# Attention heads in pairs on halves of the array, with the distance term in a loaded table

## The chip, the cores and the metric

The kernel runs on one core of a Trainium2 chip. A core has a matrix engine (TensorE, in the profile PE, with its weight loads listed apart as PEld), a vector engine (VectorE, DVE), a scalar engine (ScalarE, ACT), a general engine (GpSimd, POOL), a queue engine (SyncE, SP) and 16 DMA engines. PE multiplies a stationary tile (it lies on the array's rows and columns) with a moving tile and adds into PSUM; the other engines read PSUM and work on SBUF. The metric is device time in microseconds (us).

## The reference

Two layers of a decoder, for 256 tokens of width 1024 in f32. Each layer normalizes, projects to the inputs of four token mixers, gates and merges them, and projects out; then comes a dense feed-forward (layer 0) or one with 8 experts of which each token uses 2 (layer 1). The attention is the part that matters here; `q`, `k` and `v` have 8 heads of 64:

```python
h = rmsnorm(x, norm_mix[l])
z = h @ w_in[l]
z_a, z_b, z_q, z_k, z_v, z_d = jnp.split(z, IN_SPLITS, axis=-1)
...
scores = jnp.einsum('brnqhd,brnkhd->brnqhk', qb, kk, ...) / math.sqrt(dh)
alibi = -slopes[None, :, None] * (dist * dilation).astype(jnp.float32)[:, None, :]
scores = jnp.where(valid[:, :, None, :], scores + alibi, MASK_VALUE)
m = jnp.max(scores, axis=-1, keepdims=True)
p = jnp.exp(scores - m)
den = jnp.sum(p, axis=-1)
o = jnp.einsum('brnqhk,brnkhd->brnqhd', p, vv.astype(jnp.float32)) / den[..., None]
```

This is done for three pairs of window and dilation, whose outputs are mixed by a softmax of their denominators. Over 256 tokens that is one softmax over all earlier keys, in which a key counts as often as configurations reach it: each score gets the head's distance term, −slope × distance, and the logarithm of that count (−1e30 for a count of zero).

## The kernel before, in words

**Weights.** SP loads the f32 weights in tiles of 1 MB (`raw`, L133). `split` turns each half into two rounded parts: ACT copies the high part (`whi`, L172), DVE subtracts it for the low one (`wlo`, L173). A projection in the mixers is then two matmuls per 128 × 128 block: `whi` with both parts of the activations (512 columns, L249) and `wlo` with the high one (256 columns, L251). The feed-forward stages use three matmuls (L164 to L166). PE runs these streams back to back from weight tile to weight tile.

**The mixer of a layer** (`mixer_layer`, L273) is a list of units, each of them a piece of such a projection. Two side generators are fed in between the units: `first_side` (gating unit, pooling, convolution of 31 steps) and `attention` (L465). After each unit `pump` advances them by a rate: from the sixth unit on 2.2 steps of `first_side` and 1.6 of `attention`. What comes out is a program order; a scheduler then lays out each engine's instructions from it, with waits on semaphores where tiles come free or results are needed. In the kernel before it mixes attention's matmuls one by one into the projection.

**Attention** goes head by head in a pipeline of three steps.

- `scores` (L470): for each half `t` of the queries a matmul of 64 rows, queries stationary and keys moving (L476, 128 and 256 columns), then a matmul of two rows in bf16 (L478), which adds the distance term from the small table `al` into the same PSUM. Both halves of one head share one PSUM bank (`pss`).
- `softmax` (L482): DVE scales the scores and adds `lc`, the logarithm of the count, which is a part of the tile `mc` (L484); then the row maximum (L490), the exponential on ACT (L492), the reciprocal (L494), and the scaling of the two halves. `turned` (L499) transposes the three blocks on PE (L502), and ACT copies them out (L504).
- `values` (L507): two matmuls of 64 columns (L511 with 256 moving columns, L513 with 128). Even heads write PSUM rows 0 to 63, odd heads rows 64 to 127 of the same tile `po`.

Heads of even number lie on rows 0 to 63 of the `qT` and `kT` tiles, those of odd number on rows 64 to 127. In the loop of L518 head `i` has its scores taken while head `i − 1` is turned and head `i − 2` meets its values. The PSUM tiles of attention come from a pool with four banks.

**Small tables.** `small_loads` (L282) issues on POOL's queue, once for each layer, the small parameters (`sm`, L284), four more and `mc` (L290), in layer 0 also `al` and `cst`. After them POOL masks a part of `sm` (L303), while DVE halves a bias from it (`hb`, L301).

Of the kernel before, what the change touches and what calls it, by code (L numbers as in the profile page):

```python
# [2 lines left out]

# [2 lines left out]

# [4 lines left out]

F32 = mybir.dt.float32
F32R = mybir.dt.float32r
BF16 = mybir.dt.bfloat16
I32 = mybir.dt.int32
AF = mybir.ActivationFunctionType
ALU = mybir.AluOpType
# [2 lines left out]
P = 128  # L20
D = 1024
T = 256
# [3 lines left out]
HEADS = 8  # L26
HD = 64
# [15 lines left out]
C_LT = C_IOTA + 256  # L43
C_KEY = C_LT + 64
C_END = C_KEY + 8
M_LC = 0
M_PA = M_LC + 384
M_END = M_PA + 4 * 272


# [12 lines left out]
def shape_constants():  # L63
    c = np.zeros((P, C_END), np.float32)
    m = np.zeros((P, M_END), np.float32)
    i = np.arange(P)

    q = np.arange(T)[:, None]
    k = np.arange(T)[None, :]
    dist = q - k  # L70
    cnt = np.zeros((T, T))
    for window, dil in ((128, 1), (512, 4), (2048, 16)):
        cnt += (dist >= 0) & (dist <= window) & (dist % dil == 0)
    lc = np.where(cnt > 0, np.log(np.maximum(cnt, 1)), -1e30).astype(np.float32)
    m[:, M_LC:M_LC + 128] = lc[:P, :P]
    m[:, M_LC + 128:M_LC + 384] = lc[P:]
# [15 lines left out]
    al = np.zeros((P, 3, T), ml_dtypes.bfloat16)  # L92
    for h in range(HEADS):
        s = 8.0 * 2.0 ** (-8.0 * (h + 1) / HEADS)
        o = 32 * (h % 4)
        al[o, h // 4] = -s * np.arange(T)
        al[o + 1, h // 4] = s
        al[o, 2] = 1.0
        al[o + 1, 2] = np.arange(T)
    return c, m, al  # L100


@with_exitstack
def decoder_kernel(ctx, tc, x_in, consts_in, mconsts_in, alibi_in, small_in, gln_in, gbs_in, norms_in, w_in,
                   w_br_a, w_br_b, w_br_c, w_br_d, w_gate, w_out, dense_w1, dense_w3, dense_w2,
                   router_in, moe_w, out):
    nc = tc.nc
    cp = ctx.enter_context(tc.tile_pool(name="cp", bufs=1))
# [4 lines left out]
    psB = ctx.enter_context(tc.tile_pool(name="psB", bufs=4, space=bass.MemoryType.PSUM))  # L113
# [57 lines left out]
    def split(hi, lo, src):  # L171
        return (nc.scalar.activation(hi, src, AF.Copy),  # L172
                nc.vector.tensor_tensor(out=lo, in0=src, in1=hi.bitcast(F32), op=ALU.subtract))  # L173


    x = cp.tile([P, TT, D], F32, name="x")
# [17 lines left out]
    al = cp.tile([P, 3, T], BF16, name="al")  # L194

    def sqrt_table(after, rows=slice(None)):

# [75 lines left out]
    def mixer_layer(l, h):  # L273
        with ExitStack() as lctx:
# [7 lines left out]
            def small_loads():  # L282
                q = nc.gpsimd
# [5 lines left out]
                                        ap=[[0, 64], [1, P]]))  # L289
                q.dma_start(mc, mconsts_in)  # L290
                if l == 0:
                    q.dma_start(al, alibi_in)
                    q.dma_start(cst, consts_in)

            mean_w = lp.tile([P, P], F32, name="mean_w")
# [168 lines left out]

            def attention():  # L465
                yc = y_tile("c", 4, "yc", "y4", 1)
                lc = mc[:, M_LC:M_LC + 384]
                po = None

                def scores(hd):  # L470
                    j, r = hd // 2, slice((hd % 2) * 64, (hd % 2) * 64 + 64)
                    ps = psB.tile([P, 384], F32, name="pss", tag="ax")
                    for t in range(TT):
                        o = ps[:, 0:128] if t == 0 else ps[:, 128:384]
                        nk = P * (t + 1)
                        nc.tensor.matmul(o, lhsT=qT[r, j, t * P:(t + 1) * P], rhs=kT[r, j, 0:nk], start=True, stop=False)  # L476
                        ar = slice(32 * (hd % 4), 32 * (hd % 4) + 2)
                        nc.tensor.matmul(o, lhsT=al[ar, hd // 4, t * P:(t + 1) * P], rhs=al[ar, 2, 0:nk],  # L478
                                         start=False, stop=True)
                    return ps  # L480

                def softmax(ps):  # L482
                    s = wk.tile([P, 384], F32, name="s", tag="s", bufs=2)
                    nc.vector.scalar_tensor_tensor(out=s, in0=ps, scalar=1.0 / math.sqrt(HD), in1=lc,  # L484
                                                   op0=ALU.mult, op1=ALU.add)
                    nm = wk.tile([P, TT], F32, name="nm", tag="nm", bufs=3)
                    den = wk.tile([P, TT], F32, name="den", tag="den", bufs=3)
# [16 lines left out]
                    nc.scalar.activation(pr, pT, AF.Copy)  # L504
                    return pr

                def values(hd, pr, po):  # L507
                    r = slice((hd % 2) * 64, (hd % 2) * 64 + 64)
                    if po is None:
                        po = psB.tile([P, T], F32, name="po", tag="ax")  # L510
                    nc.tensor.matmul(po[r, :], lhsT=v[:, 0, hd * HD:(hd + 1) * HD], rhs=pr[:, 0:256],  # L511
                                     start=True, stop=False, skip_group_check=True)
                    nc.tensor.matmul(po[r, 128:256], lhsT=v[:, 1, hd * HD:(hd + 1) * HD], rhs=pr[:, 256:384],  # L513
                                     start=False, stop=True, skip_group_check=True)
                    if hd % 2 == 1:
                        split(yc[0][:, hd // 2], yc[1][:, hd // 2], po)
                        po = None
                    return po  # L518

                ps, sf, pr = {}, {}, {}  # L520
                for i in range(HEADS + 2):
                    if i >= 2:
                        po = values(i - 2, pr.pop(i - 2), po)
                        yield
                    if 1 <= i <= HEADS:
                        pr[i - 1] = turned(sf.pop(i - 1))
                        yield
                    if i < HEADS:
                        sf[i] = softmax(scores(i))
                        yield  # L530

            def evac_v(t, ps):
                nc.scalar.activation(v[:, t], ps, AF.Copy)
# [63 lines left out]
            order[13:13] = [(lambda: branch_unit("a", w_br_a, 2, True, False), (2.2, 1.6))]  # L597
            order[18:18] = [(lambda: branch_unit("b", w_br_b, 2, False, False), (2.2, 1.6))]
            for un, r in order:
                un()  # L600
                pump(*r)
# [445 lines left out]
    ps = None  # L1047
# [8 lines left out]
def layouts(inputs):  # L1056

    f = {k: np.ascontiguousarray(np.asarray(v)) for k, v in inputs.items()}
    L = DEPTH
    consts, mconsts, alibi = shape_constants()  # L1060
    small = np.empty((L, P, S_END), np.float32)
    for l in range(L):
        s = small[l]
# [16 lines left out]
    moe_w = np.ascontiguousarray(np.concatenate(tiles, axis=3))  # L1080
    gln = np.stack([f["gmlp_ln_g"], f["gmlp_ln_b"]], axis=1).reshape(L, 512)
    return {
        "x": f["x"][0], "consts": consts, "mconsts": mconsts, "alibi": alibi, "small": small, "gln": gln, "gbs": f["gmlp_b_s"],
        "norms": norms, "w_in": f["w_in"], "w_br_a": f["w_br_a"], "w_br_b": f["w_br_b"], "w_br_c": f["w_br_c"],
        "w_br_d": f["w_br_d"], "w_gate": f["w_gate"], "w_out": f["w_out"], "dense_w1": f["dense_w1"],
        "dense_w3": f["dense_w3"], "dense_w2": f["dense_w2"], "router": f["moe_router"], "moe_w": moe_w,
# [21 lines left out]
```

## Time and profile before

| | before |
|---|---|
| median of 3 runs | 1617.06 us (1616.21 to 1619.08) |
| profiled execution | 1616.96 us |
| its span | 1615.1 us |
| granted clock of PE, mean | 0.987 |
| matmuls of attention in the two layers | L476 and L478: 32 each; L511 and L513: 16 each; transposes L502: 48 (of L476, L511 and L513, in plain f32, the profile lists two passes each) |

The span is what the profiler sees between the first and the last instruction; the time of an execution has a little around it. In rows of the page's groups an engine and a line are followed by output and inputs, by partitions × elements, the count, busy time, the mean of one in ns, and the idle time before them. In rows in order of time the first two numbers are start and length in us. Ends of matmuls are modelled and overlap the next start, so lengths on PE are read from start to start. Layer 0's output projection begins at 229.6 us, and that of layer 1 follows some 432 us behind; the expert stage takes the time from about 700 us to the end.

### The profile page before, as it was taken

What the parts mean: (1) busy time and instruction counts of PE and PEld (TensorE: products, weight loads), DVE (VectorE), ACT (ScalarE), POOL (GpSimd) and SP (SyncE); (2) the same over time, 40 slices, a digit from 0 to 9 for tenths busy, and PEclk for the clock granted to TensorE, in tenths of its full rate; (3) what the DMA queues carried; (4) which work ended last, traced back from release to release, by engine and by line L of the source; (5) the groups of instructions that cost most, each with busy time, mean ns of one, the idle gap of its engine ahead of it and who ended that gap; (6) DMA issues with size and microseconds to landing.
All of it is one profiled execution on the core that took longest, in us unless ns stands there. A gap on an engine that the chain in (4) does not pass through costs nothing.

```text
span 1615.1 us, 20045 instructions
## 1 busy us (share of the span) xinstructions
PE 1556.3 (96%) x7540; PEld 1077.2 (67%) x7540; DVE 978.8 (61%) x1291; ACT 811.4 (50%) x1184; POOL 12.3 (1%) x32
## 2 busy tenths in 40 slices
PE   6999999999999999999999999999999999999996
PEld 5888897888878788886556555556555555565553
DVE  5885776656579767765545574555654545644544
ACT  5566655555565667545444443445434444544342
POOL 1000000000000000000000000000000000000000
PEclk9999999999999999979999999999999999999998
DMA  9654455556565544649999989999989999899993
GB/s 309 188 178 133 155 169 184 183 185 192 170 210 165 161 143 157 236 176 384 407 420 412 368 349 421 412 390 383 410 363 405 405 403 378 330 423 415 399 395 129
DMA packets 133929, 472.05 MB, mean 292 GB/s; under 512 B 7504, under 2 KB 77136, under 8 KB 90816
## 3 DMA queue, kind: packets, MB, share of 16 engines
q1 hardware_dynamic: 132512, 466.65, 75.5%
q0 software_dynamic: 1024, 3.52, 0.6%
q8 instruction: 61, 1.00, 0.3%
q10 hardware_dynamic: 288, 0.52, 0.1%
q14 instruction: 44, 0.36, 0.1%
HBM read 469.61 MB, written 1.05 MB: 291 GB/s over the span
## 4 chain that ended last, share of the span: by engine, by line
PE 89%; DVE 4%; ACT 4%; issue 2%; DMA 1%; SPq 0%; DVEq 0%; ACTq 0%; POOL 0%; POOLq 0%
PE psw L249 16%; PE psq L929 13%; PE psw L251 8%; PE psu L165 7%; PE psu L166 6%; PE psu L164 6%; PE psds L950 5%; PE psd L165 3%; ACT whi L172 3%; DVE wlo L173 3%; PE psd L166 3%; PE psd L164 2%; PE psg L841 2%; PE psf L164 1%; PE psf L165 1%
## 5 line engine op out<-in xcount | busy, mean ns | idle before, releaser
L173 DVE TENSOR_TENSOR wlo<-raw,whi 128x1024 fp32r<-128x1024 f32 x546 | 647.6, 1221 | 259.8 <-ACT whi L172 257.0
L172 ACT ACTIVATE whi<-raw 128x1024 fp32r<-128x1024 f32 x546 | 554.2, 1053 | 134.5 <-PE psw L249 47.2
L249 PE MATMUL psw<-hp,whi 128*128 128x512 f32 x1088 | 388.9, 400 | 0.4 <-DVE hp L173 0.4
L251 PE MATMUL psw<-hp,wlo 128*128 128x256 f32 x1088 | 307.4, 283 | 0.0
L249 PEld LDWEIGHTS psw<-hp,whi 128*128 128x128 f32 x1088 | 204.8, 188 | 51.7 <-DVE hp L173 0.8
L929 PE MATMUL psq<-raw,xs 128*64 128x512 f32 x896 | 218.6, 596 | 0.0
L251 PEld LDWEIGHTS psw<-hp,wlo 128*128 128x128 f32 x1088 | 205.9, 189 | 3.0 <-issue 1.8
L165 PE MATMUL psu<-wlo,xer 128*128 128x512 f32 x448 | 182.8, 408 | 9.5 <-DVE wlo L173 9.5
L164 PE MATMUL psu<-whi,xer 128*128 128x512 f32 x448 | 179.0, 400 | 1.3 <-DVE x L908 1.2
L166 PE MATMUL psu<-whi,xel 128*128 128x512 f32 x448 | 175.6, 392 | 0.0
L929 PEld LDWEIGHTS psq<-raw,xs 128*64 128x64 f32 x896 | 65.3, 137 | 129.0 <-issue 128.7
L931 ACT ACTIVATE gfs<-psq 64x512 f32<-64x512 f32 x28 | 16.5, 591 | 250.6 <-PE psq L929 250.6
L165 PEld LDWEIGHTS psu<-wlo,xer 128*128 128x128 f32 x448 | 84.3, 188 | 63.7 <-issue 30.8
L164 PEld LDWEIGHTS psu<-whi,xer 128*128 128x128 f32 x448 | 84.5, 189 | 41.8 <-ACT whi L172 17.0
L950 PE MATMUL psds<-raw,gTs 128*64 128x512 f32 x448 | 110.0, 604 | 0.0
L932 DVE TENSOR_TENSOR gfs<-gfs,psq 64x512 f32<-64x512 f32 x28 | 19.4, 691 | 138.5 <-ACT gfs L931 138.5
L166 PEld LDWEIGHTS psu<-whi,xel 128*128 128x128 f32 x448 | 84.5, 189 | 15.1
L165 PE MATMUL psd<-wlo,gTr 128*128 128x512 f32 x224 | 92.3, 412 | 2.2
L166 PE MATMUL psd<-whi,gTl 128*128 128x512 f32 x224 | 88.2, 394 | 0.0
L268 ACT ACTIVATE sum<-psw 128x256 f32<-128x256 f32 x120 | 44.9, 374 | 69.9 <-PE psw L251 69.9
L878 ACT ACTIVATE gfm<-psu 128x512 f32<-128x512 f32 x28 | 16.7, 597 | 122.5 <-PE psu L166 122.5
L164 PE MATMUL psd<-whi,gTr 128*128 128x512 f32 x224 | 75.4, 413 | 2.9 <-ACT whi L172 2.9
(264 smaller groups left out, 1610.4 us busy)
## 6 DMA issues: line engine op xcount, KB each, us to landing
raw<-in_moe_w_dram SPq DMA_DIRECT2D x336, 1024.0 KB, 8.4
raw<-in_dense_w_dram SPq DMA_DIRECT2D x33, 1024.0 KB, 5.3
raw<-in_w_gate_dram SPq DMA_DIRECT2D x32, 1024.0 KB, 5.8
raw<-in_w_in_dram SPq DMA_DIRECT2D x22, 1024.0 KB, 5.6
raw<-in_w_out_dram SPq DMA_DIRECT2D x8, 1024.0 KB, 4.9
raw<-in_w_br_c_dram SPq DMA_DIRECT2D x4, 1024.0 KB, 5.0
gain<-in_norms_dram SPq DMA_DIRECT2D x5, 512.0 KB, 4.2
raw<-in_w_br_a_dram SPq DMA_DIRECT2D x2, 1024.0 KB, 4.9
```

What stands on the lines that cost most here:

```text
L164: nc.tensor.matmul(ps, lhsT=lhs[0], rhs=rhs[0], start=start, stop=False)
L165: nc.tensor.matmul(ps, lhsT=lhs[0], rhs=rhs[1], start=False, stop=False)
L166: nc.tensor.matmul(ps, lhsT=lhs[1], rhs=rhs[0], start=False, stop=stop)
L172: return (nc.scalar.activation(hi, src, AF.Copy), nc.vector.tensor_tensor(out=lo, in0=src, in1=hi.bitcast(F32), op=ALU.subtract))
L173: nc.vector.tensor_tensor(out=lo, in0=src, in1=hi.bitcast(F32), op=ALU.subtract))
L249: nc.tensor.matmul(ps.rearrange("p a t -> p (a t)"), lhsT=w[0], rhs=act[:, k].rearrange("p a t -> p (a t)"), start=start, stop=False)
L251: nc.tensor.matmul(ps[:, 1], lhsT=w[1], rhs=act[:, k, 0], start=False, stop=stop)
L268: nc.scalar.activation(out[:, b], ps[b][:, 1], AF.Copy)
L841: nc.tensor.matmul(ps[:, b, cs], lhsT=ht[part][:, t, k * P:(k + 1) * P], rhs=self.G[:, t].rearrange("p s n -> p (s n)")[:, cs], start=n == ...
L929: nc.tensor.matmul(ps[rows], lhsT=xs[:, kk], rhs=w[:, k], start=kk == 0, stop=kk == KD - 1)
L932: nc.vector.tensor_tensor(out=gf[HI], in0=gf[HI], in1=ps[HI], op=ALU.mult)
L950: nc.tensor.matmul(acc["s"][rows], lhsT=gT[:, 2 * j + k], rhs=w[:, k, n * 512:(n + 1) * 512], start=c == 0 and j == 0 and k == 0, stop=c = ...
```

## The change

**Scores by pairs.** `scores` now takes a pair of heads and two PSUM banks. For each half of the queries it issues the matmul of the even head, on rows 0 to 63, then that of the odd head, on rows 64 to 127 and into the other bank. The bf16 matmuls of L478 and the table `al` are gone.

**Distance in a table.** The host lays the sum of `lc` and the distance term out for each head, 8 tables of 128 × 384 f32 (192 KB). `bias` loads a head's table by POOL's queue into the tile `s` that the softmax then works in (four buffers where there were two), and the first operation adds it from there (`in1=s`). `mc` loses its first 384 of 1472 columns.

**Values by pairs.** The four matmuls of a pair stand together: 256 columns for the even head (PSUM rows 0 to 63) and the odd one (rows 64 to 127), then 128 columns for each.

**Rates.** The loop runs over pairs, with a step after each head's softmax, one after a pair is turned and one after its values, and the rate of `attention` is 1.2 steps a unit instead of 1.6.

```diff
-                    ps = psB.tile([P, 384], F32, name="pss", tag="ax")
+                def scores(pair):
+                    ps = [psB.tile([P, 384], F32, name="pss", tag="ax") for _ in range(2)]
                     for t in range(TT):
-                        o = ps[:, 0:128] if t == 0 else ps[:, 128:384]
-                        nk = P * (t + 1)
-                        nc.tensor.matmul(o, lhsT=qT[r, j, t * P:(t + 1) * P], rhs=kT[r, j, 0:nk], start=True, stop=False)
-                        ar = slice(32 * (hd % 4), 32 * (hd % 4) + 2)
-                        nc.tensor.matmul(o, lhsT=al[ar, hd // 4, t * P:(t + 1) * P], rhs=al[ar, 2, 0:nk],
-                                         start=False, stop=True)
+                        c, nk = (slice(0, 128) if t == 0 else slice(128, 384)), P * (t + 1)
+                        for i, r in enumerate((slice(0, HD), slice(HD, P))):
+                            nc.tensor.matmul(ps[i][:, c], lhsT=qT[r, pair, t * P:(t + 1) * P], rhs=kT[r, pair, 0:nk],
+                                             start=True, stop=True)
                     return ps
-                def softmax(ps):
-                    s = wk.tile([P, 384], F32, name="s", tag="s", bufs=2)
-                    nc.vector.scalar_tensor_tensor(out=s, in0=ps, scalar=1.0 / math.sqrt(HD), in1=lc,
+                def bias(hd):
+                    b = wk.tile([P, 384], F32, name="s", tag="s", bufs=4)
+                    nc.gpsimd.dma_start(b, bias_in[hd])
+                    return b
+                def softmax(ps, s):
+                    nc.vector.scalar_tensor_tensor(out=s, in0=ps, scalar=1.0 / math.sqrt(HD), in1=s,
...
-                def values(hd, pr, po):
-                    r = slice((hd % 2) * 64, (hd % 2) * 64 + 64)
...
+                def values(pair, pr):
+                    po = psB.tile([P, T], F32, name="po", tag="ax")
+                    for t, c in enumerate((slice(0, T), slice(P, T))):
+                        for i in range(2):
+                            hd = 2 * pair + i
+                            nc.tensor.matmul(po[i * HD:(i + 1) * HD, c], lhsT=v[:, t, hd * HD:(hd + 1) * HD],
+                                             rhs=pr[i][:, t * T:t * T + T - t * P], start=t == 0, stop=t == 1,
+                                             skip_group_check=True)
+                    split(yc[0][:, pair], yc[1][:, pair], po)
...
-            order = [(un, r) for un, r in zip(units, [(2, 0)] * 5 + [(2.2, 1.6)] * 16)]
+            order = [(un, r) for un, r in zip(units, [(2, 0)] * 5 + [(2.2, 1.2)] * 16)]
```

**What moves on PE.** Scores of layer 0 in the kernel before, with the projection (`psw`) around them and transposes (L502) of the head ahead in between; names end in the tile's number:

```order
L249 MATMUL psw_954<-hp_92,whi_946 128x512
L502 MATMUL pT_863<-ident_77,s_796 128x128 [waits Activation_49]
L476 MATMUL pss_869<-kT_158,qT_157 128x128
L502 MATMUL pT_863<-ident_77,s_796 128x128 [waits Activation_49]
L502 MATMUL pT_863<-ident_77,s_796 128x128
L478 LDWEIGHTS al_89
L478 MATMUL pss_869<-al_89 128x128
L476 MATMUL pss_869<-kT_158,qT_157 128x256
L478 LDWEIGHTS al_89
L478 MATMUL pss_869<-al_89 128x256
L251 MATMUL psw_954<-hp_92,wlo_947 128x256
```

After the change, the second pair of layer 0 on PE (L464 is the score matmul, L240 and L242 the projection):

```order
L242 MATMUL psw_970<-hp_91,wlo_950 128x256
L464 MATMUL pss_1002<-kT_157,qT_156 128x128
L464 MATMUL pss_1003<-kT_157,qT_156 128x128
L464 MATMUL pss_1002<-kT_157,qT_156 128x256
L464 MATMUL pss_1003<-kT_157,qT_156 128x256
L240 MATMUL psw_1030<-hp_91,whi_1022 128x512 [waits DVE_49]
```

A head's scores were six instructions between others; a pair's now are four in a row, the two heads in turn.

The values of a pair of layer 0 after the change, also on PE:

```order
L242 MATMUL psw_1115<-hp_91,wlo_1095 128x256
L504 MATMUL po_1143<-pr_935,v_158 64x256
L504 MATMUL po_1143<-pr_941,v_158 64x256
L504 MATMUL po_1143<-pr_935,v_158 64x128
L504 MATMUL po_1143<-pr_941,v_158 64x128
L240 MATMUL psw_1172<-hp_91,whi_1164 128x512 [waits DVE_49]
```

Before, the two matmuls of one head stood in the projection, and those of the other head came some 70 instructions later.

**What moves on POOL.** The small tables of layer 1 before; `DMASW` are its DMA queues, the other names in brackets the engines waited for:

```order
L296 MEMSET mean_w_4018 128x128 [waits DVE_49,PE_49,Pool_49]
L325 MEMSET cpad_4027 128x2x30 [waits Pool_49]
L284 DMA sm_4014<-in_small_dram 128x744 [waits DMASW1_49,Pool_49]
L285 DMA gln_4015<-in_gln_dram 128x512 [waits DMASW2_49]
...
L290 DMA mc_4017<-in_mconsts_dram 128x1472 [waits DMASW7_49]
L303 AFFINE_SELECT sm_4014<-sm_4014 128x512 [waits DMASW1_49]
```

And after, with the tables of attention (`s`, L471) on the same queue:

```order
L471 DMA s_4855<-in_bias_dram 128x384 [waits DVE_49,DMASW2_49,PE_49,Activation_49]
L471 DMA s_4857<-in_bias_dram 128x384 [waits DVE_49,DMASW3_49,PE_49,Activation_49]
L286 MEMSET mean_w_4008 128x128 [waits DVE_49,PE_49,Pool_49]
L315 MEMSET cpad_4017 128x2x30 [waits Pool_49]
L275 DMA sm_4004<-in_small_dram 128x744 [waits DVE_49,DMASW4_49,Activation_49,Pool_49]
L276 DMA gln_4005<-in_gln_dram 128x512 [waits DMASW5_49,Activation_49]
...
L281 DMA mc_4007<-in_mconsts_dram 128x1088 [waits DMASW2_49,DVE_49]
L293 AFFINE_SELECT sm_4004<-sm_4004 128x512 [waits DMASW4_49]
L471 DMA s_5074<-in_bias_dram 128x384 [waits DVE_49,DMASW3_49,PE_49,Activation_49]
```

The tables of pairs 0 and 1 of layer 1 (four issues) now stand ahead of the small loads, those of pairs 2 and 3 behind them. The semaphores of `mean_w` stand for other work than before: it waited for PE's last matmul of the down projection of layer 0's feed-forward and now waits for an earlier gate product (`gl`) on DVE and for a matmul of the mixer; `sm` now waits itself, for the last gate product's first part (`gf`, L648 before) and the last `sil` on ACT.

More of the change, by code (lines that the diff above doesn't have):

```diff
@@ L45 @@
 C_END = C_KEY + 8
-M_LC = 0
-M_PA = M_LC + 384
+M_PA = 0
 M_END = M_PA + 4 * 272
@@ L74, in shape_constants @@
     lc = np.where(cnt > 0, np.log(np.maximum(cnt, 1)), -1e30).astype(np.float32)
-    m[:, M_LC:M_LC + 128] = lc[:P, :P]
-    m[:, M_LC + 128:M_LC + 384] = lc[P:]
+    bias = np.zeros((HEADS, P, 384), np.float32)
+    for h in range(HEADS):
+        b = lc - (2.0 ** (-8.0 * (h + 1) / HEADS) * dist).astype(np.float32)
+        bias[h, :, 0:128] = b[:P, :P]
+        bias[h, :, 128:384] = b[P:]
     t = np.arange(T)
@@ L90, in shape_constants, with decoder_kernel @@
     c[:, C_LT:C_LT + 64] = (e[None, :] < e[:, None]).reshape(1, 64)
[L92 to L100, printed above, removed]
+    return c, m, bias
 @with_exitstack
-def decoder_kernel(ctx, tc, x_in, consts_in, mconsts_in, alibi_in, small_in, gln_in, gbs_in, norms_in, w_in,
+def decoder_kernel(ctx, tc, x_in, consts_in, mconsts_in, bias_in, small_in, gln_in, gbs_in, norms_in, w_in,
                    w_br_a, w_br_b, w_br_c, w_br_d, w_gate, w_out, dense_w1, dense_w3, dense_w2,
@@ L505, in turned @@
                     return pr
-                def values(hd, pr, po):
-                    r = slice((hd % 2) * 64, (hd % 2) * 64 + 64)
[L509 to L518, printed above, removed]
@@ L522, in attention @@
+                sf, pr = {}, {}
+                npair = HEADS // 2
+                for i in range(npair + 2):
                     if i >= 2:
-                        po = values(i - 2, pr.pop(i - 2), po)
+                        values(i - 2, pr.pop(i - 2))
                         yield
-                    if 1 <= i <= HEADS:
-                        pr[i - 1] = turned(sf.pop(i - 1))
+                    if 1 <= i <= npair:
+                        pr[i - 1] = [turned(s) for s in sf.pop(i - 1)]
@@ L527, in attention @@
                         yield
-                    if i < HEADS:
-                        sf[i] = softmax(scores(i))
-                        yield
+                    if i < npair:
+                        bs = [bias(2 * i + j) for j in range(2)]
+                        ps = scores(i)
+                        sf[i] = []
+                        for j in range(2):
+                            sf[i].append(softmax(ps[j], bs[j]))
+                            yield
             def evac_v(t, ps):
@@ L594, in pump @@
                         next(sd[0], None)
[L596 to L598 removed]
+            order = [(un, r) for un, r in zip(units, [(2, 0)] * 5 + [(2.2, 1.2)] * 16)]
+            order[13:13] = [(lambda: branch_unit("a", w_br_a, 2, True, False), (2.2, 1.2))]
+            order[18:18] = [(lambda: branch_unit("b", w_br_b, 2, False, False), (2.2, 1.2))]
             for un, r in order:
@@ L1059, in layouts @@
     L = DEPTH
-    consts, mconsts, alibi = shape_constants()
+    consts, mconsts, bias = shape_constants()
     small = np.empty((L, P, S_END), np.float32)
@@ L1082, in layouts @@
     return {
-        "x": f["x"][0], "consts": consts, "mconsts": mconsts, "alibi": alibi, "small": small, "gln": gln, "gbs": f["gmlp_b_s"],
+        "x": f["x"][0], "consts": consts, "mconsts": mconsts, "bias": bias, "small": small, "gln": gln, "gbs": f["gmlp_b_s"],
         "norms": norms, "w_in": f["w_in"], "w_br_a": f["w_br_a"], "w_br_b": f["w_br_b"], "w_br_c": f["w_br_c"],
```

10 lines of the change are left out of this document (removed).

## The prediction

> **What bounds the kernel now.** I read the page first, then busy time by stretch, then the instructions around the attention matmuls in order of time.
>
> ```profile
> span 1615.1 us, 20045 instructions
> PE 1556.3 (96%) x7540; PEld 1077.2 (67%) x7540; DVE 978.8 (61%) x1291; ACT 811.4 (50%) x1184; POOL 12.3 (1%) x32
> PE 89%; DVE 4%; ACT 4%; issue 2%; DMA 1%; SPq 0%; DVEq 0%; ACTq 0%; POOL 0%; POOLq 0%
> 60.00:117.00 57.00, 57.00 (x323) 46.31 (x322) 52.55 (x104) 32.66 (x60) 0.00 (x0) 1.00 0.54 163
> 117.00:210.00 93.00, 93.00 (x541) 76.30 (x540) 60.65 (x100) 61.92 (x123) 0.00 (x0) 1.00 0.48 148
> ```
>
> TensorE (PE) is 89% of the chain that ended last. The two stretches hold layer 0's attention; their columns are length, then busy time of PE, weight loads, DVE, ACT and POOL, the granted clock, DMA share and GB/s. PE is busy in every microsecond at clock 1.00, DMA at half load: here a microsecond taken from PE is one off the end, as long as its suppliers keep up. DVE, at 52.55 of 57.00, is the one to watch. Layer 1 repeats this 432 us later.
>
> **What attention costs PE now.** Matmuls are pipelined, so I count from start to start. Undisturbed, the projection stream goes L249, 0.24 us, L251, 0.12 us, L249. Whatever stands between is charged from the start the next one would have had, plus the wider first step after it.
>
> One head's scores alone, in the order of time on PE:
>
> ```profile
> 91.54 0.40 PE L249 MATMUL psw<-hp,whi 128*128 128x512 f32 x1
> 91.78 0.28 PE L251 MATMUL psw<-hp,wlo 128*128 128x256 f32 x1
> 91.98 0.48 PE L476 MATMUL pss<-kT,qT 64*128 64x128 f32 x2
> ...
> 93.18 0.28 PE L478 MATMUL pss<-al 2*128 2x256 bf16 x1
> 93.39 0.50 PE L249 MATMUL psw<-hp,whi 128*128 128x512 f32 x1
> 93.73 0.28 PE L251 MATMUL psw<-hp,wlo 128*128 128x256 f32 x1
> ```
>
> L249 would have come at 91.90 and came at 93.39, its step is 0.34 instead of 0.24: 1.49 + 0.10 = 1.59 us. Next, scores mixed with the previous head's three transposes; one head's values; scores and values in a row; one transpose:
>
> ```profile
> 105.50 0.39 PE L249 MATMUL psw<-hp,whi 128*128 128x512 f32 x1
> ...
> 107.71 0.39 PE L251 MATMUL psw<-hp,wlo 128*128 128x256 f32 x1
> 107.94 0.39 PE L249 MATMUL psw<-hp,whi 128*128 128x512 f32 x1
> ...
> 111.11 0.39 PE L249 MATMUL psw<-hp,whi 128*128 128x512 f32 x1
> 111.44 0.65 PE L511 MATMUL po<-pr,v 128*64 128x256 f32 x2
> ...
> 112.23 0.39 PE L251 MATMUL psw<-hp,wlo 128*128 128x256 f32 x1
> 112.45 0.40 PE L249 MATMUL psw<-hp,whi 128*128 128x512 f32 x1
> ...
> 156.60 0.28 PE L251 MATMUL psw<-hp,wlo 128*128 128x256 f32 x1
> ...
> 159.02 0.50 PE L249 MATMUL psw<-hp,whi 128*128 128x512 f32 x1
> 159.35 0.28 PE L251 MATMUL psw<-hp,wlo 128*128 128x256 f32 x1
> ...
> 166.18 0.39 PE L249 MATMUL psw<-hp,whi 128*128 128x512 f32 x1
> 166.41 0.27 PE L502 MATMUL pT<-ident,s 128*128 128x128 f32 x1
> 166.44 0.36 PE L251 MATMUL psw<-hp,wlo 128*128 128x256 f32 x1
> 166.64 0.39 PE L249 MATMUL psw<-hp,whi 128*128 128x512 f32 x1
> ```
>
> Mixed: 107.71 − 105.74 + 0.11 = 2.08. Values: 112.23 − 111.35 + 0.10 = 0.98. In a row: 159.02 − 156.72 + 0.10 = 2.40. A transpose costs 0.03 + 0.08 = 0.11, three of them 0.33. By the order of PE's instructions a layer has one scores alone, four mixed, three in a row and five values alone. Without transposes, which stay: 1.59 + 4 × (2.08 − 0.33) + 3 × 2.40 + 5 × 0.98 = 20.7 us per layer.
>
> **What it costs after.** The distance matmuls (L478) are gone, and each pair's four score matmuls stand together, as do the four of values, alternating between halves of the array. Whether halves run at the same time is seen where the kernel uses them already:
>
> ```profile
> 73.06 1.08 PE L409 MATMUL psp<-pooled,sm 64*64 64x256 f32 x8
> 74.08 0.39 PE L251 MATMUL psw<-hp,wlo 128*128 128x256 f32 x1
> ...
> 734.91 7.09 PE L929 MATMUL psq<-raw,xs 128*64 128x512 f32 x32
> 741.93 0.50 PE L164 MATMUL psd<-whi,gTr 128*128 128x512 f32 x1
> ...
> 948.20 0.73 PE L905 MATMUL pssc<-ys,GT 64*128 64x512 f32 x4 [0.69 <-ACT ys L172]
> ```
>
> The last is row halves: the trace view merges four 512-wide passes into 0.73 us. L929 alternates column halves: 32 passes in 7.02 us (734.91 to the next matmul at 741.93), 0.22 each. L409 alternates both: eight 256-wide passes in 74.08 − 73.06 = 1.02. An f32 matmul is two passes; four of them, two at a time, make four slots of 0.213 (a quarter of L929's pair time, 0.43 for 512 columns, gives the same per column) and 0.16 of start and drain.
>
> A pair's scores are 128 and 256 columns for two heads at once: 0.64 of slots by that rate, 0.16 start and drain, an allowance of 0.10 for a longer first step (my estimate, from the step of 0.34 instead of 0.24 that the stream takes after a change of shape), and 0.19 for the gap ahead and the wide step after, as above: 1.09 us where two heads took at least 3.18. Values have the same columns: 0.64 + 0.16 + 0.19 = 0.99, about what one head takes now. Per layer 4 × (1.09 + 0.99) = 8.3; saved 20.7 − 8.3 = 12.4, in two layers **24.8 us**.
>
> **What is only moved.** ACT and DVE do the same work per head. The bias loads are sixteen issues on POOL, which has nothing else there. In the order, tables of pairs 0 and 1 of layer 0 go out after the small loads, those of layer 1 during layer 0, and those of pairs 2 and 3 as soon as the tiles of pairs 0 and 1 have been transposed, some 50 projection steps of 0.36, about 18 us, ahead of their use.
>
> ```profile
> al<-in_alibi_dram POOLq DMA_DIRECT2D x1, 192.0 KB, 9.6
> 10.00:20.00 10.00, 4.66 (x15) 3.08 (x14) 5.88 (x10) 5.68 (x11) 0.73 (x2) 1.00 1.05 377
> 2.20 13.73 DMA raw<-in_w_in_dram
> ```
>
> The slowest landing of a table of this size took 9.6 us, so 18 us cover it. At the start DMA is the bound: the first weights land at 15.93. Four tables (0.79 MB) come, `al` and a part of `mc` (0.39 MB) go; 0.4 MB at 377 GB/s is 1.0 us at most, zero at least as they are issued behind the weights. I take +0.3, since most of it lands after PE has begun.
>
> In layer 1 the small loads change place:
>
> ```profile
> 443.59 3.40 DMA sm<-in_small_dram
> 447.01 1.01 DVE L301 TENSOR_SCALAR hb<-sm 128x32 f32<-128x32 f32 x1 [1.17 <-DMA sm<-in_small_dram]
> 447.32 0.67 POOL L303 TENSOR_SCALAR_AFFINE_SELECT sm<-sm 128x512 f32<-128x512 f32 x1
> ```
>
> This wait is on the chain. The smaller `mc` moves the tiles, and the wait of `sm` in the new program is that of the last gate product, some 7 us earlier, not that of the last down projection. DVE loses up to `hb`'s 1.17 of waiting and most of its 1.01, of which transposes and ACT's copy hide much: −0.5, between 0 and −1.2.
>
> Row and rule: `hb` ran 1.01 us until POOL's L303 ended. [...]
>
> In the expert layer the scheduler's order differs in places, with the same instructions and the same order of weight loads. What there is to win or lose:
>
> ```profile
> PE psu L165 <- DVE wlo L173: 9.5, 16, 0.6
> ```
>
> A third of that either way, ±3; I take 0.
>
> **Sum.** The profiled execution took 1616.96 (span 1615.1, 1.9 around it; the median of the runs is 1617.06). 1616.96 − 24.8 + 0.3 − 0.5 = 1592.0.
>
> **Rivals.** *Halves run one after the other.* Then 0.64 is added per pair to scores, or to values, or both: 8 × 0.64 = 5.1 each, 1597 or 1602. Against it stand L929 and L905; for it, that neither is f32 on row halves alone. [...]
>
> *DVE becomes the bound.* Pairs bring their softmax sooner: two more heads fall in the stretch up to 117 us.
>
> ```profile
> L484 DVE SCALAR_TENSOR_TENSOR s<-pss,mc 128x384 f32<-128x384 f32 x16 | 8.7, 546 | 7.2 <-PE pss L478 7.0
> L490 DVE TENSOR_REDUCE nm<-s 128x1 f32<-128x256 f32 x16 | 6.5, 408 | 0.0
> L490 DVE TENSOR_REDUCE nm<-s 128x1 f32<-128x128 f32 x16 | 4.4, 278 | 0.0
> ```
>
> At 1.2 us each, 2.5 more on 52.55, in a stretch that gets about 1.8 shorter: 55.0 of 55.2, full. If the weight splits (L173) come late for it, up to 4 us per layer are lost: 1600. For it is that sum; against it, that DVE has a third free from 117 on, and that the convolution, not the splits, can lag.
>
> *Slower: the table is late.* The softmax's first DVE operation now waits for a POOL DMA; behind it on DVE wait the splits, and behind these PE. Pairs 2 and 3 of each layer are exposed, four times. It is slower once these lose 28 us, 7 per pair, so from a landing of 18 + 7 = 25 us on; at 30 us it is 1592 + 4 × 12 = 1640. The longest landing seen speaks against it.
>
> *It does nothing*, if PE waits elsewhere for what it gains: 1617. With no PE idle time in either stretch I see no place for it.
>
> **Chances.** Forecast, 1587 to 1597 around 1592: 0.74. More gain, by the expert layer's order: 0.05. Halves in turn (1597 to 1602): 0.08. DVE (to 1600): 0.08. Nothing: 0.02. Late table: 0.03. The range 1586 to 1601 holds the first and most of the next three. Changes under 0.2% (3.2 us) can't be told here: faster 0.95, same 0.02, slower 0.03.
>
> **What would show it.** Right: no L478; the score and value matmuls in groups of eight passes, 0.9 and 0.8 us long, passes of two heads starting together; PE still without idle time in both layers' attention; out projection of layer 0 starting 12 us earlier; `hb` of layer 1 without a DMA wait. Wrong: passes of a pair 0.2 apart one by one; PE waiting for L173's results before 117 us; the softmax's first operation waiting for the bias DMA.

## The result

The changed kernel takes 1590.65 us (median of 4 runs, 1589.61 to 1592.21), the kernel before 1618.07 us beside it (4 runs, 1616.21 to 1619.26). The ratio is 0.9832, with a 95% interval from 0.9821 to 0.9844: 27.4 us less. The forecast was 1592.0 in a range from 1586 to 1601. The profiled execution took 1589.84 us.

The page of the changed kernel, as shown of the one before: its span, the busy time of the engines, and the chain that ended last by engine.

```profile
span 1588.1 us, 20024 instructions
PE 1531.3 (96%) x7508; PEld 1065.8 (67%) x7508; DVE 977.8 (62%) x1291; ACT 808.1 (51%) x1184; POOL 20.8 (1%) x47
PE 89%; DVE 4%; ACT 4%; issue 2%; DMA 1%; SPq 0%; DVEq 0%; ACTq 0%
```

PE lost 25.0 us of busy time and is still 89% of the chain; the other engines did what they did before. POOL's 8.5 us more are in the main the 16 issues of tables, 0.54 us each, where the one of `al` went. The two stretches with layer 0's attention (length, then busy time of PE, weight loads, DVE, ACT and POOL, clock, DMA share, GB/s):

```profile
60.00:117.00 57.00, 57.00 (x336) 47.41 (x333) 54.16 (x110) 34.12 (x63) 1.10 (x2) 1.00 0.54 172
117.00:210.00 93.00, 93.00 (x613) 81.85 (x612) 68.56 (x108) 64.17 (x128) 3.23 (x6) 1.00 0.55 180
```

PE is busy in every microsecond as before. In the same 93 us it now does 613 passes where it did 541. What a pair costs is read from start to start, as in the prediction: first a pair's scores (L464), then a pair's values (L504), in the order of time on PE.

```profile
91.21 0.28 PE L242 MATMUL psw<-hp,wlo 128*128 128x256 f32 x1
91.41 0.93 PE L464 MATMUL pss<-kT,qT 64*128 64x128 f32 x8
92.27 0.50 PE L240 MATMUL psw<-hp,whi 128*128 128x512 f32 x1
92.61 0.28 PE L242 MATMUL psw<-hp,wlo 128*128 128x256 f32 x1
...
122.21 0.28 PE L242 MATMUL psw<-hp,wlo 128*128 128x256 f32 x1
122.42 0.87 PE L504 MATMUL po<-pr,v 128*64 128x256 f32 x8
123.22 0.50 PE L240 MATMUL psw<-hp,whi 128*128 128x512 f32 x1
```

L240 would have come at 91.21 + 0.12 = 91.33 and came at 92.27, and its step is 0.34 instead of 0.24: 92.27 − 91.33 + 0.10 = 1.04 us for a pair's scores (1.09 forecast). Values: 123.22 − 122.33 + 0.10 = 0.99 (0.99 forecast).

To see where the 27 us come from I cut both traces at the same work: the first matmul of the pooling (`psp`) and the first of the output projection (`pso`), in layer 0 and layer 1. Before:

```profile
67.27 0.47 PE L400 MATMUL psp<-mc,zb 128*64 128x144 f32 x4
229.56 0.39 PE L164 MATMUL pso<-whi,mp 128*128 128x512 f32 x1
498.78 0.47 PE L400 MATMUL psp<-mc,zb 128*64 128x144 f32 x4
661.07 0.39 PE L164 MATMUL pso<-whi,mp 128*128 128x512 f32 x1
```

After the change:

```profile
66.69 0.47 PE L390 MATMUL psp<-mc,zb 128*64 128x144 f32 x4
216.30 0.39 PE L156 MATMUL pso<-whi,mp 128*128 128x512 f32 x1
485.09 0.47 PE L390 MATMUL psp<-mc,zb 128*64 128x144 f32 x4
634.47 0.39 PE L156 MATMUL pso<-whi,mp 128*128 128x512 f32 x1
```

With the first and last matmul of the feed-forward's down projection (`psf`) and the first of the expert stage (`psu`) as further cuts, the stages are these. The fourth column is a second trace of the changed kernel, from the run c1 below.

| stage, us | before | changed | changed, again | forecast of the difference |
|---|---|---|---|---|
| start to pooling, layer 0 | 67.27 | 66.69 | 66.61 | +0.3 |
| pooling to output projection, layer 0 (attention) | 162.29 | 149.61 | 149.61 | −12.4 |
| output projection to first down projection | 51.39 | 52.52 | 52.68 | 0 |
| down projections | 161.80 | 161.83 | 161.86 | 0 |
| last down projection to pooling, layer 1 | 56.03 | 54.44 | 55.69 | −0.5 |
| pooling to output projection, layer 1 (attention) | 162.29 | 149.38 | 149.38 | −12.4 |
| output projection to expert stage | 50.19 | 49.25 | 50.19 | 0 |
| expert stage to the end of the span | 903.9 | 904.4 | 904.8 | 0 |

The two attention stages hold 12.68 + 12.91 = 25.6 us of it, to 0.01 us the same in both traces of the changed kernel. The other stages move by up to 1.6 us, and by up to 1.3 us between two traces of one program.

### The profile page after: what moved, and what is told of

It reads as the page before. It is cut to its first block, busy times and chain, and to the rows that moved or that the text cites. A ratio compares the mean times of both kernels' runs of the same rounds, so it can differ in the third digit from the quotient of the medians.

```text
span 1588.1 us, 20024 instructions
## 1 busy us (share of the span) xinstructions
PE 1531.3 (96%) x7508; PEld 1065.8 (67%) x7508; DVE 977.8 (62%) x1291; ACT 808.1 (51%) x1184; POOL 20.8 (1%) x47
## 3 DMA queue, kind: packets, MB, share of 16 engines
HBM read 472.17 MB, written 1.05 MB: 298 GB/s over the span
## 4 chain that ended last, share of the span: by engine, by line
PE 89%; DVE 4%; ACT 4%; issue 2%; DMA 1%; SPq 0%; DVEq 0%; ACTq 0%
PE psw L240 16%; PE psq L923 14%; PE psw L242 8%; PE psu L157 7%; PE psu L158 7%; PE psu L156 6%; PE psds L944 5%; PE psd L157 3%; ACT whi L164 3%; PE psd L158 3%; DVE wlo L165 3%; PE psd L156 2%; PE psg L835 2%; PE psf L156 1%; PE psf L158 1%
## 5 line engine op out<-in xcount | busy, mean ns | idle before, releaser
L240 PE MATMUL psw<-hp,whi 128*128 128x512 f32 x1088 | 388.6, 400 | 0.6 <-DVE hp L165 0.6
L242 PE MATMUL psw<-hp,wlo 128*128 128x256 f32 x1088 | 307.0, 282 | 0.0
L240 PEld LDWEIGHTS psw<-hp,whi 128*128 128x128 f32 x1088 | 205.1, 188 | 52.8 <-issue 3.3
L242 PEld LDWEIGHTS psw<-hp,wlo 128*128 128x128 f32 x1088 | 206.3, 190 | 2.1 <-issue 1.1
```

The source lines that it names most:

```text
L240: nc.tensor.matmul(ps.rearrange("p a t -> p (a t)"), lhsT=w[0], rhs=act[:, k].rearrange("p a t -> p (a t)"), start=start, stop=False)
L242: nc.tensor.matmul(ps[:, 1], lhsT=w[1], rhs=act[:, k, 0], start=False, stop=stop)
```

## The experiments

My theory: PE is the bound in attention, and a pair costs what it does because matmuls on the two halves of the array run at the same time. Against it stood that the halves run in turn and the table alone makes the gain, that DVE becomes the bound, and that a late table holds DVE up.

**The change itself again (c1).** No edit.

> The changed kernel itself once more, beside the three that follow, so that they are compared on one chip, and for a second trace of the same program: 27 us under the kernel before. If the clock that PE is granted after the normalizations falls at another moment in this trace, that part of a difference between two kernels (about 1 us per normalization) is no work of the change.

Measured: 1591.48 us (1590.30 to 1592.57) against 1617.37, ratio 0.9836 (0.9819 to 0.9852). Its trace is the fourth column of the table. The stage ahead of layer 1's pooling took 1.25 us longer than in the first trace, with the same instructions; the section on the clock comes back to it.

**Table alone (e1).** The kernel before with `bias`, `in1=s` and the narrower `mc`, and without L478:

```diff
...
-                        nc.tensor.matmul(o, lhsT=al[ar, hd // 4, t * P:(t + 1) * P], rhs=al[ar, 2, 0:nk],
-                                         start=False, stop=True)
...
```

> The kernel before, head by head, with the distance tables of the change and without the bf16 matmuls (L478); nothing is paired. My theory: what a bf16 matmul stood for on PE goes, 0.15 + 0.21 = 0.36 us per head in the trace of before, 16 heads 5.8 us, and hb of layer 1 loses its DMA wait as in the changed kernel (1.6 us): 1618.1 - 7.4 = 1610.7. The rival that the gain of the change comes mostly from taking the bf16 matmuls out, and that the halves run in turn: 20 us or more, 1598 or less.

Measured: 1608.27 us (1606.65 to 1608.44) against 1619.56, ratio 0.9932 (0.9915 to 0.9948). One head's scores in its trace, in the order of time on PE:

```profile
91.40 0.28 PE L245 MATMUL psw<-hp,wlo 128*128 128x256 f32 x1
91.61 0.92 PE L468 MATMUL pss<-kT,qT 64*128 64x128 f32 x4
92.46 0.50 PE L243 MATMUL psw<-hp,whi 128*128 128x512 f32 x1
```

92.46 − 91.52 + 0.10 = 1.04 us where one head with its distance matmuls took 1.59, and **to 0.01 us what a pair of heads takes in the changed kernel**. The attention stages took 158.71 us each, 3.6 less than before: the bf16 matmuls cost 0.45 us a head on the mean and not 0.36, and 0.55 where a head's scores stood alone. So in the attention stages the table is worth 7.2 us when it stands alone, and the rival that it makes most of the gain falls. The total fell by some 11 us, as the ratio says; the other 4 lie in stages that also vary between traces of one program, and no run puts them down to the table.

**Pairs without the table (e2).** The changed kernel with the distance term back as four bf16 matmuls behind the two heads' scores, the wide `mc` and no tables loaded:

```diff
...
+                        for i in range(2):
+                            hd = 2 * pair + i
+                            ar = slice(32 * (hd % 4), 32 * (hd % 4) + 2)
+                            nc.tensor.matmul(ps[i][:, c], lhsT=al[ar, hd // 4, t * P:(t + 1) * P], rhs=al[ar, 2, 0:nk],
+                                             start=False, stop=True)
...
```

> The changed kernel with the distance term back in bf16 matmuls, four per pair behind the two heads' score matmuls, and no tables loaded. My theory: half to all of 0.36 us per head comes back, 2.9 to 5.8 us, and with the wide constants tile the DMA wait of hb (1.6): 1590.7 + 4.5 to 7.4 = 1595 to 1598. The rival that tables make the gain: 1610 or more. In the profile the score group should take 1.2 to 1.6 us where it took 0.86.

Measured: 1599.85 us (1598.76 to 1601.43) against 1619.56, ratio 0.9886 (0.9869 to 0.9902), some 2 us above what I expected; of the 9 us to the changed kernel the attention stages give 4.7 and the wait of `hb` 0.5, the rest lies in the stages that vary. A pair's scores in the order of time on PE:

```profile
91.87 0.28 PE L251 MATMUL psw<-hp,wlo 128*128 128x256 f32 x1
92.08 0.49 PE L474 MATMUL pss<-kT,qT 64*128 64x128 f32 x4
92.50 0.23 PE L479 MATMUL pss<-al 2*128 2x128 bf16 x2
92.66 0.70 PE L474 MATMUL pss<-kT,qT 64*128 64x256 f32 x4
93.30 0.28 PE L479 MATMUL pss<-al 2*128 2x256 bf16 x2
93.51 0.50 PE L249 MATMUL psw<-hp,whi 128*128 128x512 f32 x1
```

One head alone before:

```profile
91.98 0.48 PE L476 MATMUL pss<-kT,qT 64*128 64x128 f32 x2
92.40 0.22 PE L478 MATMUL pss<-al 2*128 2x128 bf16 x1
92.55 0.70 PE L476 MATMUL pss<-kT,qT 64*128 64x256 f32 x2
93.18 0.28 PE L478 MATMUL pss<-al 2*128 2x256 bf16 x1
93.39 0.50 PE L249 MATMUL psw<-hp,whi 128*128 128x512 f32 x1
```

The steps are, to 0.01 us, the same (0.42, 0.15, 0.63, 0.21), now for two heads. A pair takes 93.51 − 91.99 + 0.10 = 1.62 us, 0.58 more than with the table, and an attention stage 151.84, 2.2 to 2.5 more. Pairs alone (with the new rate) are thus worth 10.45 us a layer, the table alone 3.6, both together 12.7 to 12.9: where two heads share one bf16 step there is less left for the table to save.

**Both heads on the same rows (e3).**

```diff
-                        for i, r in enumerate((slice(0, HD), slice(HD, P))):
+                        for i, r in enumerate((slice(0, HD), slice(0, HD))):
```

> The changed kernel with both heads of a pair taking queries and keys from rows 0 to 63, so that odd heads get the even heads' scores; the instructions are the same in number, shape and order. My theory (row halves run at the same time): eight passes in a row instead of two at a time, 0.64 us more per pair, 8 pairs 5.1 us: 1595.8, and the score group takes 1.5 instead of 0.86 us. The rival that the halves run in turn already: no change, 1590.7.

The total, 3805.78 us, tells nothing: with other scores the router sends tokens elsewhere, and the expert stage does other work (3108 us instead of 904, with 45149 instructions in the whole trace instead of 20024). The answer is in layer 0, whose instructions are those of the changed kernel; in the order of time on PE:

```profile
92.53 0.28 PE L242 MATMUL psw<-hp,wlo 128*128 128x256 f32 x1
92.73 1.57 PE L464 MATMUL pss<-kT,qT 64*128 64x128 f32 x8
94.24 0.50 PE L240 MATMUL psw<-hp,whi 128*128 128x512 f32 x1
```

94.24 − 92.65 + 0.10 = 1.69 us instead of 1.04: 0.65 more, where 0.64 was expected. The attention stages took 151.91 us, 2.3 and 2.5 more.

**Both heads on the same columns (e5).**

```diff
-                    po = psB.tile([P, T], F32, name="po", tag="ax")
+                    po = psB.tile([P, 2, T], F32, name="po", tag="ax")
...
-                            nc.tensor.matmul(po[i * HD:(i + 1) * HD, c], lhsT=v[:, t, hd * HD:(hd + 1) * HD],
+                            nc.tensor.matmul(po[0:HD, i, c], lhsT=v[:, t, hd * HD:(hd + 1) * HD],
...
```

> The changed kernel with the values of both heads of a pair on columns 0 to 63 of the array, in two places of one PSUM bank; each half is then evacuated by itself (one more ACT and one more DVE instruction per pair), and the result is the same. My theory (column halves run at the same time): the group of values takes 0.80 + 0.64 = 1.44 us, 5.1 us more over 8 pairs. The rival that column halves run in turn already: the group stays at 0.80 us and the time does not change.

Other than the expectation says, the values are no longer the attention's with both heads' sums in one bank on the same rows (why, no run shows), so here too the total (3814.62 us) is that of another expert stage. In the order of time on PE, layer 0:

```profile
122.65 0.28 PE L242 MATMUL psw<-hp,wlo 128*128 128x256 f32 x1
122.86 1.51 PE L504 MATMUL po<-pr,v 128*64 128x256 f32 x8
124.30 0.50 PE L240 MATMUL psw<-hp,whi 128*128 128x512 f32 x1
```

124.30 − 122.77 + 0.10 = 1.63 us instead of 0.99: 0.64 more, as expected. The attention stages took 152.85 us each, 3.2 and 3.5 more, which is above the sum of the groups; in the second pair of layer 0 one of the four matmuls also stands apart (141.73 and 144.56 us), and the rest of it was not followed up. So both kinds of halves run at the same time, and this is 4 × (0.65 + 0.64) = 5.2 us of the 12.8 of a layer.

**Head by head within the group (e4).** The same four matmuls, the even head's two first:

```diff
-                    for t in range(TT):
-                        for i, r in enumerate((slice(0, HD), slice(HD, P))):
+                    for i, r in enumerate((slice(0, HD), slice(HD, P))):
+                        for t in range(TT):
```

(and the same in `values`).

> The changed kernel with the matmuls of a pair still in one group, but first those of the even head, then those of the odd head, for scores and for values. My theory (a pass starts with the one ahead of it only if that one is on the other half): only the last pass of the even head and the first of the odd one overlap, 0.53 us more per group, 16 groups 8.5 us: 1599.2. The rival that standing together in one group makes the gain, not the alternation: no change, 1590.7.

Measured: 1590.32 us (1589.28 to 1591.17) against 1619.56, ratio 0.9825 (0.9809 to 0.9842). I expected 8.5 us more and got none. Its attention stages took 149.88 and 150.14 us, 0.3 and 0.8 more; in the second pair of layer 0 one of the values' matmuls stands apart from the other three (140.13 and 142.53 us). In the order of time on PE, layer 0:

```profile
90.92 0.28 PE L242 MATMUL psw<-hp,wlo 128*128 128x256 f32 x1
91.13 0.93 PE L464 MATMUL pss<-kT,qT 64*128 64x128 f32 x8
91.99 0.50 PE L240 MATMUL psw<-hp,whi 128*128 128x512 f32 x1
```

91.99 − 91.04 + 0.10 = 1.05 us, against 1.04. In the records of the single passes all four passes of 128 columns start ahead of the four of 256, in twos 0.013 us apart (0.007 in the changed kernel), although the order of PE's instructions is 128, 256 (even head), 128, 256 (odd head). The odd head's first matmul did not wait for the even head's second. My theory of a strict order falls: what counted here is that the matmuls stand in one group (0.86 us from the first start to the next matmul, as in the changed kernel), not that they alternate.

**The old rate (e8).**

```diff
-            order = [(un, r) for un, r in zip(units, [(2, 0)] * 5 + [(2.2, 1.2)] * 16)]
+            order = [(un, r) for un, r in zip(units, [(2, 0)] * 5 + [(2.2, 1.6)] * 16)]
...
```

> The changed kernel with the old rate of 1.6 attention steps a unit. In the order of PE's instructions the second and third pair's four score matmuls then stand between transposes of the pair ahead (one transpose, one score matmul, two transposes, three score matmuls), two of four pairs have their values taken apart, and softmax work on DVE comes earlier. My theory (a full-height transpose between them ends the overlap of two heads, and DVE has room): 0.3 to 0.6 us for each of these eight places, 2.5 to 5 us more than the changed kernel, with PE never idle from 60 to 210 us. The rival that DVE becomes the bound when softmax comes earlier: PE waits for the weight splits before 117 us, 8 us more or worse.

Measured: 1598.29 us (1597.00 to 1598.46) against 1617.69, ratio 0.9873 (0.9856 to 0.9889). The second pair's scores on PE, mixed with transposes (L493):

```profile
107.87 0.40 PE L240 MATMUL psw<-hp,whi 128*128 128x512 f32 x1
108.11 0.27 PE L493 MATMUL pT<-ident,s 128*128 128x128 f32 x1
108.31 0.48 PE L464 MATMUL pss<-kT,qT 64*128 64x128 f32 x2
108.72 0.44 PE L493 MATMUL pT<-ident,s 128*128 128x128 f32 x2
109.09 0.92 PE L464 MATMUL pss<-kT,qT 64*128 64x128 f32 x6
109.94 0.38 PE L242 MATMUL psw<-hp,wlo 128*128 128x256 f32 x1
```

109.94 − 108.11 + 0.10 − 0.33 for the transposes = 1.60 us instead of 1.04: 0.56 lost, within the 0.3 to 0.6 expected. The first stretch of attention, in the columns as above:

```profile
60.00:117.00 57.00, 57.00 (x331) 46.23 (x330) 54.23 (x110) 35.05 (x69) 1.10 (x2) 1.00 0.54 170
```

The attention stages took 152.25 and 152.27 us, 2.6 and 2.9 more, a little above the expected sum. So the rate of 1.2 is part of the gain, 5.5 us of it in this order of instructions, because it keeps other instructions out of the groups (seen here in one of them). DVE is as full as in the changed kernel (54.23 of 57), and PE never idle: the rival of DVE falls here too. The rest of the difference to the changed kernel (about 6 us by the ratios) lies in the stages that vary.

**Two buffers for the tables (e7).**

```diff
-                    b = wk.tile([P, 384], F32, name="s", tag="s", bufs=4)
+                    b = wk.tile([P, 384], F32, name="s", tag="s", bufs=2)
```

> The changed kernel with two buffers instead of four for the tables: a pair's tables are then issued only once the pair ahead has been transposed, some 10 projection steps (3.5 us) before its scores instead of a whole pair earlier, and they take 4.2 us to land. The first softmax operation should wait 1 to 3 us on DVE for them, in 7 of the 8 pairs. My theory that DVE has room for it: 0 to 4 us more. The rival of the prediction (DVE waits, the splits behind it are late, PE stops): each wait comes through to PE, 7 us or more.

Measured: 1589.80 us (1589.05 to 1590.71) against 1617.37, ratio 0.9830 (0.9813 to 0.9846). Its tables take 2.5 to 6.2 us from issue to landing, and the group of the softmax's first operation says that none was waited for (the last column is idle time):

```profile
L475 DVE SCALAR_TENSOR_TENSOR s<-pss,s 128x384 f32<-128x384 f32 x16 | 8.6, 550 | 0.1
```

The waits that I expected did not come: the order of DVE's instructions now has the second head's operation 2.7 us behind the first's (111.95 and 114.67 in the second pair), with other work between. The tables that two buffers hold back were issued 4.9 to 13.4 us ahead of their use, and the closest landed 0.4 us before it. So four buffers are not needed here, and the price of a table that is really late was not measured.

**The width of the constants (e6).**

```diff
-M_PA = 0
+M_PA = 384
```

> The changed kernel with the constants tile mc at its old width of 1472 columns (the first 384 unused). My theory that the smaller tile moves sm to memory that comes free earlier, which takes the DMA wait from hb in layer 1: hb waits again, and the second half of the normalization is turned 0.5 us later, up to 1.6 us with the clock that follows it. The rival that the place of the small loads on the POOL queue does it: hb starts without a wait, and nothing changes.

Measured: 1591.07 us (1589.82 to 1594.14) against 1617.37, ratio 0.9842 (0.9826 to 0.9858). In its trace `hb` waits again:

```profile
434.28 0.22 DVE L291 TENSOR_SCALAR hb<-sm 128x32 f32<-128x32 f32 x1 [1.22 <-DMA sm<-in_small_dram]
```

In the changed kernel it does not:

```profile
433.66 0.18 DVE L291 TENSOR_SCALAR hb<-sm 128x32 f32<-128x32 f32 x1
```

From the last down projection to the first matmul of layer 1's projection it is 8.14 us here, 8.10 before, and 7.56 and 7.57 in the two traces of the changed kernel; e1 with the narrow `mc` has 7.64, e2 with the wide one 8.10. So the smaller `mc` takes the wait away, and that is worth 0.54 us, too little to be told from the total.

**The clock held (e9).** The second trace of the changed kernel differed from the first by 1.25 us in a stage whose work is the same. The granted clock tells why. Here are the stretches behind the normalization ahead of layer 1 and at the entry of the expert stage in the first trace (the clock is the third number from the end):

```profile
436.26:439.67 3.41, 3.05 (x12) 2.79 (x13) 2.01 (x4) 1.67 (x3) 0.00 (x0) 0.50 0.39 141
440.00:443.00 3.00, 3.00 (x15) 2.44 (x14) 2.83 (x3) 2.98 (x4) 0.00 (x0) 1.00 0.01 3
667.00:690.00 23.00, 22.02 (x95) 20.68 (x96) 13.88 (x44) 6.57 (x13) 0.00 (x0) 0.55 0.45 183
```

and in the second:

```profile
435.69:442.52 6.83, 5.80 (x18) 4.96 (x19) 5.17 (x7) 4.42 (x6) 0.00 (x0) 0.50 0.22 77
440.00:443.00 3.00, 3.00 (x9) 2.34 (x9) 2.74 (x4) 3.00 (x4) 0.00 (x0) 0.58 0.05 20
667.00:690.00 23.00, 20.70 (x87) 19.77 (x88) 14.02 (x47) 5.67 (x12) 0.00 (x0) 0.52 0.45 183
```

In both traces PE idles 2.12 us, transposes for 1.3 us and idles 2.17 us more; in the second gap its clock falls to half, for 3.4 us in the first trace and 6.8 in the second. At the entry of the expert stage it has half its clock for 20.5 and 23.9 us. So I filled the gaps:

```diff
+    def fill(n, rhs, after=None):
+        w = psA.tile([P, 256], F32, name="fill", tag="mm")
+        if after is not None:
+            nc.tensor.matmul(w[0:16], lhsT=after.rearrange("p a b -> p (a b)"), rhs=rhs, start=True, stop=True)
+        for _ in range(n):
+            nc.tensor.matmul(w, lhsT=ident, rhs=rhs, start=True, stop=True)
...
+                if ps is not None and t == 0 and n == 1:
+                    fill(4, hh[:, 0, 512:768])
...
+                if t == 1:
+                    fill(3, hT[1][:, 0], lg)
...
+            fill(1, hT[1][:, 0], sel)
```

> The changed kernel with matmuls whose results nobody reads (f32, 256 columns, 0.43 us each) in places where PE is idle: four between the two halves of each normalization ahead of the feed-forward and of layer 1's mixer, four in the routing after the logits and two after the expert counts. In the traces of the changed kernel PE is granted half its clock from such a gap on, for 3 to 7 us after a normalization and for about 20 us at the entry of the expert stage. My theory that this half clock costs time and comes from the idle gap: the clock stays at 1.00 there, the stretch from the last down projection to layer 1's pooling takes 53 us instead of 54.4 or 55.7, that from the output projection to the down projection 50.5 instead of 52.6, and the entry of the expert stage is up to 9 us shorter: 5 to 12 us less, 1579 to 1586. The rival that the clock falls whatever runs there, or that the short matmuls of the gather keep it low: 0 to 2 us less, or slower by the work added.

Measured: 1584.90 us (1583.69 to 1586.04) against 1617.69, ratio 0.9795 (0.9779 to 0.9811). The same places:

```profile
437.00:440.00 3.00, 3.00 (x15) 2.47 (x14) 2.75 (x4) 3.00 (x4) 0.00 (x0) 1.00 0.44 175
440.00:443.00 3.00, 3.00 (x15) 2.48 (x14) 3.00 (x4) 2.80 (x4) 0.00 (x0) 1.00 0.30 65
667.00:690.00 23.00, 22.54 (x126) 19.44 (x126) 18.33 (x43) 14.54 (x21) 0.00 (x0) 0.93 0.65 251
```

What the clock is worth shows in the first 32 short matmul passes at the entry of the expert stage (`psg`), at 0.50 in the first trace of the changed kernel and then at 1.00 here:

```profile
669.31 7.06 PE L835 MATMUL psg<-G,htp 128*128 128x128 f32 x32 [0.71 <-DVE cmp L749]
667.44 3.87 PE L848 MATMUL psg<-G,htp 128*128 128x128 f32 x32
```

The stage from output projection to down projection took 50.80 us (52.5 to 52.7 in the changed kernel), the one ahead of layer 1's pooling 53.27 (54.4 and 55.7), and that to the expert stage 43.57 (49.2 and 50.2). The expert stage gave 1 to 2 us back (906.0). By the ratios this kernel is about 6 us faster than the changed one, and its interval lies below both of that one's (0.9821 to 0.9844, 0.9819 to 0.9852). It beats both kernels.

## Why the prediction was right

**Attention.** Its sum held by its own terms: 1.04 instead of 1.09 us for a pair's scores, 0.99 as forecast for its values, so 4 × 2.03 = 8.1 us a layer where 20.7 went before. That gives 12.6 us; the stages show 12.7 and 12.9, the forecast was 12.4. The allowance of 0.10 for a longer first step was too much by half, which is 0.4 us in two layers. (Where the prediction says a quarter of L929's pair time of 0.43, it is half, 256 of 512 columns: 0.215, against the 0.213 of the sum.)

**What makes it up.** The prediction put down the difference without dividing it. By the experiments a layer's 12.8 us are 5.2 from the halves running at the same time (e3, e5), 2.2 to 2.5 from the table (e2), and the remaining 5, as I read it, from fewer separate insertions into the projection. That part is the rest of a sum and was not measured by a run of its own; e8 can't give it, since a head's matmul of 128 columns alone between transposes took 0.41 us there (108.31 to 108.72), as long as those of two heads in e2 (0.42). With the table counted first (3.6, e1) the rest is 4. The halves that L409, L929 and L905 showed were the right rows to judge by.

**`hb`.** Forecast −0.5, measured −0.54, and by the mechanism named (e6: a wait of 1.22 us with the wide `mc`, none with the narrow one). That the stage fell by 1.59 in the first trace and only by 0.34 in the second goes with the clock: it was at half for 3.4 us in the first, for 6.8 in the second, and for 6.8 before (447.6 to 454.4), as these stretches of the kernel before show:

```profile
447.00:451.00 4.00, 1.75 (x9) 1.78 (x10) 2.76 (x6) 0.79 (x2) 0.98 (x2) 0.57 0.69 232
451.00:454.00 3.00, 3.00 (x9) 2.32 (x9) 2.57 (x4) 2.77 (x4) 0.00 (x0) 0.50 0.48 157
454.00:457.00 3.00, 3.00 (x14) 2.44 (x13) 3.00 (x4) 1.65 (x3) 0.00 (x0) 0.93 0.20 23
```

**The start.** Forecast +0.3. The nine traces of kernels with pairs and tables (alike up to layer 0's pooling but for e6's wide `mc` and e7's two tables) took between 66.35 and 68.02 us to it (67.27 before), so the term is below what can be seen.

**The expert stage.** Forecast 0 ± 3, measured +0.5 and +1.0, with 902.4 for e4, whose code there is the same: it varies by that much from run to run.

**The rivals.** Halves in turn: fallen (e3, e5; two heads now take what e1 takes for one). DVE as the bound: fallen; of the 2.5 us expected in the stretch up to 117 us, 1.6 came (54.16 instead of 52.55), and PE was never idle. Table late: the landings were short of the 18 us of room by far,

```profile
DMA to landing us min/median/max: 2.5/4.2/6.5
```

and the exposed ones were issued 23 to 30 us ahead of their use. e7 shows that 4.9 us of room did no harm either (no wait, 0.1 us idle). The forecast of 1592.0 against 1590.65 is nearer than its terms: attention was 0.8 us better than forecast, and the start and the clock went the right way by chance in the profiled execution.

## What to carry to other kernels

Read the price of small matmuls inside a stream from the start the stream would have had to the start it got: here two matmuls of two rows cost 0.55 us where a head's scores stood alone (e1). Gather small matmuls of independent halves of the array in one group with nothing of full height between them: a pair's scores took 1.04 us so, as much as one head's in e1, and 1.60 with transposes in between, the transposes' own price left out (e8). Before a stage's microsecond is explained, look at a second trace of the same program, and at the granted clock. Where the clock falls behind idle gaps on the chain (here to 0.50 behind two of 2.1 and 2.2 us close together; with the second one filled it held at 1.00), matmuls that nobody reads may be worth more than what they cost (about 6 us for all the places filled in e9).

## What the runs showed of the hardware

**Matmuls started out of their order.** In e4's records an odd head's matmul on rows 64 to 127 started 0.013 us behind the even head's first, with the even head's second matmul, which is ahead of it in the program, 0.33 us later; likewise with column halves. The groups took no longer for it: 0.86 us of scores and 0.81 of values from the first start to the next matmul, where the changed kernel has 0.86 and 0.80. For its values on column halves the trace lists eight weight loads of 0.13 to 0.14 us each from 122.42 to 123.05, beside the eight passes, which start from 122.42 on; the next matmul came at 123.22.

**The clock moved between runs of one program.** Behind the same idle gaps (2.12 and 2.17 us) the half clock lasted 3.4 us in one trace and 6.8 in the other (436.3 to 439.7, 435.7 to 442.5). At the entry of the expert stage the half clock lasted 20.5 us in the first trace (668.4 to 688.8), through 14.4 us of short matmuls, which kept PE busy, and 5 us of wide ones behind them. In e9 the clock came in at 1.00, stayed there for the 8.6 us that the same short matmuls took, and was at half for 3.4 us behind them.
